# One layer's core kernel: attention rows turned over 128 partitions, two weight quarters loaded into exponential tiles, and an output projection whose last half runs in two groups of four blocks

## The chip, the cores and the metric

The kernel runs on one core of a Trainium2 chip. A core has five engines with an instruction stream each: TensorE (PE) for matrix products, VectorE (DVE), ScalarE (ACT), GpSimd (POOL) and SyncE (SP), which here issues the DMA transfers. The metric is the device time of one execution in microseconds, the median of several runs.

## The reference, cut to what matters

One decoder layer for 1024 tokens of width 1024, float32. One input projection feeds two kinds of heads, four heads each, and their outputs go through one output projection and a squared-ReLU MLP:

```python
h = rms_norm(x, norm1_w)
proj = h @ w_in                     # differential attention q, k, v | DeltaNet q, k, v, gate, a, b
da_q, da_k = per-head rms_norm of 64 columns each (4 heads x 2 maps)
...
s = softmax over the causal keys of q.k / 8, two maps a head
da_o = (s1 - lambda * s2) @ da_v    # per block of 128 queries
...
dn_o = gated delta rule, chunks of 64 tokens, one state a head
mix = concat(da_o, dn_o)            # 512 + 512 columns
x = x + mix @ w_out
h = rms_norm(x, norm2_w)
x = x + square(relu(h @ w_up)) @ w_down
```

## The kernel before, in words

Every large product is made of three matrix products in a rounded float type: an operand is split into a high part (`wH`, `hH`) and a remainder (`wL`, `hL`), and PE adds high by high, high by low and low by high into the same PSUM tile. A matmul of the large stages is 128 x 128 by 128 x 512.

The order in time: the gate projections and the DeltaNet projections (to about 211 us of the span), then a long stretch in which many things run between one another (about 211 to 606 us), then the up projection and the down projection (to the end at 1225 us). The change lies in the long stretch. It holds:

- `horner` and `scan`: the chunked delta rule, with many small matmuls. `horner` keeps four 128 x 1024 tiles in the pool `ae` (four buffers, tag `pexp`; two of these tiles are called `gb` in the profile) until its last step. Its loads from DRAM are `gb`, the scan's are `pka`, `pkb` and `zgt`.
- `da_units`: the projection of the differential attention's queries, keys and values, in three units of 512 columns. A unit goes over the eight blocks of 128 tokens in four pairs, and for each pair over two halves of the 1024 input rows (`kh`); a half is four products deep and each product is three matmuls (lines 1012 to 1014). The tile `ps_qk` of a block is copied out by ACT into `qn` (line 1040; in the units with values also line 1034 or 1035), and POOL and DVE then work out its norms. When the last pair has used a half's weights, `load_unit` fetches the same half of the next unit: four quarters of 128 x 512, each in two DMAs into a tile `wraw`, of which there are two; ACT rounds each to `wH` (line 213) and DVE subtracts to get `wL` (line 214). A third quarter's DMA can therefore be issued only after the first quarter was rounded and subtracted.
- `da_turns`: the normed rows of `qn` are transposed on PE (lines 965 and 966, tile `ps_qkt`), then split into high and low part: for each half of 64 partitions ACT writes the high part into the tile `qa` at these partitions (line 972) and DVE the low part at the other 64 (line 973). Two such steps make one tile, which is written to DRAM (`qk_d`).
- `scores` and `values`: for a head, its keys are loaded from `qk_d` into two tiles `KS` (line 1068, one DMA each), and for each block its queries into `qa` (line 1085, one DMA) and, with the halves swapped, into `qb` (lines 1086 and 1087). PE forms the scores (lines 1148 to 1151), ACT the exponentials (`pexp`, line 1157, from the pool `ae` or, in part after the scan, from a pool `be`), PE turns the result (line 1189) and multiplies it with the values (line 1201).
- `mixed` and `outproj`: the output projection (lines 1291 to 1293). Its half of input rows with the DeltaNet outputs comes first, the half with the attention outputs last; the output columns come in two halves `n`. Blocks become ready one by one, from the last block to the first, since a block needs its attention outputs. For the last half the code keeps a list of (n, block) and takes the first entry that is ready; n = 1 of a block only after its n = 0. After n = 1 of a block comes `norm2`: the sums of squares (line 1310) in a tile `hn` of the pool `ae`, and a DMA `acc_d<-acc` of the block's sum to DRAM (line 1308). The same memory of the block then takes the turned rows (`kept`, line 254) of the first four blocks, and `turn_b` (line 1384) turns the other four. Once every n = 0 is done, `first_ops` loads the first operands of the up projection (`wraw<-in_w_up_dram`, line 1443; rounded at line 1371).

The order of all this is set by a planner (`Interleave`, called `flow`). Each of the above is a stream that yields the time at which it could go on; the planner picks among the streams by priority and keeps a model of the time with fixed costs (`act(n)`, `vec(n)`, `unit_time`, 2500 ns for a DMA). PE executes exactly in the planned order. The instructions of ACT, DVE, POOL and SP are ordered by the compiler's scheduler from the program, and each engine then works strictly down its own list: an instruction that waits holds up all behind it.

Of the kernel before, what the change touches and what calls it, by code (L numbers as in the profile page):

```python
# [18 lines left out]
P = 128  # L19
# [100 lines left out]
def act(n, accum=False):  # L120
    return "S", 55.0 + 0.83 * n + (93.0 if accum else 0.0)
# [11 lines left out]
def tile_hymba_layer(  # L133
# [65 lines left out]
    def load_unit(src, ranges, k0=0, nk=KB, eng=None, rp=None):  # L199
# [6 lines left out]
        for k in range(0, nk, st):  # L206
            raw = rp.tile([P, 2 * UC], F32, tag="wraw", name="wraw", bufs=5) if rp else laid("wraw")
# [563 lines left out]
    def unit_time(eng="G", rate=1230.0):  # L771
        done = []
        for i in range(4):
            start = flow.now if i < 2 else done[i - 2]
            done.append(flow.chain(("S", 520.0), (eng, rate), start=start + DMA_T))
        return done
# [180 lines left out]
    def da_turns():  # L957
        for i in range(4 * NT):
# [11 lines left out]
            for m in range(2):  # L970
                a, b = HF[m], HF[1 - m]
                S.activation(qa[a, m, :], pt[a, 0:256], AF.Copy, scale=wv[a])
                V.scalar_tensor_tensor(qa[b, m, :], pt[a, 0:256], wv[a], qa[a, m, :].bitcast(F32),
                                       ALU.mult, ALU.subtract)
            flow.pe(2 * TR)
            t = flow.chain(act(256), act(256), vec(256, 60), vec(256, 60), start=max(flow.now, qa_free[i % 2]))
            flow.put_off(t, ("qa", i % 2), lambda g=g, kind=kind, tb=tb, qa=qa: nc.sync.dma_start(
                qk_d[g, kind, tb], qa.bitcast(F32).rearrange("p m (h t) -> p m h t", h=2)))
# [8 lines left out]
    def da_units():  # L987
        todo = [[(512, 256), (0, 256)], [(1024, 256), (768, 256)], [(1280, 256), (256, 256)]]

        def half_w(src, ranges, k0):  # L990
            return load_unit(src, ranges, k0, 4, eng=V), unit_time("V", 610.0)
# [3 lines left out]
        for i in range(3):  # L995
            if i == 1:
                vts[0] = ap.tile([P, NT, P], F32, tag="vt", name="vt")
            for pair in range(NT // 2):
                pss = {}
                for kh in range(2):  # L1000
# [19 lines left out]
                    if pair == NT // 2 - 1:  # L1020
                        if i < 2:
                            w[kh] = half_w(w_in_v, todo[i + 1], 4 * kh)
# [41 lines left out]
    def load_head(h, pool):  # L1064
        KS = []
        for m in range(2):
            k = pool.tile([P, SEQ], F32R, tag=f"KS{m}", name=f"KS{m}")
            nc.sync.dma_start(k.bitcast(F32).rearrange("p (b t) -> p b t", t=P),
                              qk_d[h // 2, 1, :, :, m, h % 2, :].rearrange("b p t -> p b t"))
# [11 lines left out]
    def load_q(h, tb):  # L1081
        qa = ap.tile([P, 2, P], F32R, tag="qa", name="qa", bufs=2)
        qb = ap.tile([P, 2, P], F32R, tag="qb", name="qb", bufs=2)
        src = qk_d[h // 2, 0, tb, :, :, h % 2, :]
        nc.sync.dma_start(qa.bitcast(F32), src)
        nc.sync.dma_start(qb[HF[0]].bitcast(F32), src[HF[1]])
        nc.sync.dma_start(qb[HF[1]].bitcast(F32), src[HF[0]])
# [4 lines left out]
    ready = []  # L1092

    def scores():
# [6 lines left out]
        for u, (h, tb) in enumerate(order):  # L1101
# [31 lines left out]
            pl = n // npc  # L1133
            pe, ssum = [], ap.tile([P, 2], F32, tag="ssum", name="ssum", bufs=4)
            mx = ap.tile([P, 2], F32, tag="mx", name="mx", bufs=4)
            for m in range(2):
# [18 lines left out]
                ep = pools["be"] if state["scan"] and npe % 3 == 0 else ae  # L1155
# [699 lines left out]
```

## Time and profile before

| what | value |
|---|---|
| median of 3 runs | 1226.38 us (1225.47 to 1226.53) |
| the profiled execution | 1226.58 us, with a span of 1224.9 us |
| PE busy | 1212.0 us, 99% of the span |
| DVE, ACT, POOL busy | 850.0, 604.6, 121.0 us |
| matrix products, counted by the hardware | 6330 |
| bytes moved by DMA | 199.04 MB, mean 163 GB/s |

The span runs from the first to the last instruction of the profiled execution; the 1.7 us between it and the execution's time lie around it. Busy time of PE counts a matmul from its start to its modelled end, and successive matmuls overlap, so that the sum over the single instructions is larger than PE's busy time. In a list of waits, "PE a <- ACT b: 1.9, 1, 1.9" says that PE stood before instructions on tile a until ACT had written b, for 1.9 us in all, once, at most 1.9 us at a time. The column after POOL in a table of stretches is the TensorE clock that was granted, as a share of the full one; then come the share of the DMA engines' time that is in use, and GB/s.

### The profile page before, as it was taken

The page shows a single profiled execution, that of the slowest core. Times are in us where ns is not written, and L with a number is a line of the kernel's source. Part 1 is how long each engine was busy: PE and PEld are TensorE (multiplying, and loading weights), DVE is VectorE, ACT ScalarE, POOL GpSimd, SP SyncE. Part 2 cuts the span into 40 slices and gives each one's busy share as a digit, 9 for nine tenths or more (in the row PEclk, how much of TensorE's full clock was granted, in tenths as well). Part 3 has the DMA queues.
Part 4 walks back from the last instruction along what each step waited for, and adds up shares of the span by engine and source line. Part 5 has one row for each costly group of instructions (what it writes and reads, how often), then busy time and mean ns, then how long its engine had stood idle before and what let it go on. Part 6 is the DMA issues. An engine that isn't in the chain of part 4 may idle for free.

```text
span 1224.9 us, 17632 instructions
## 1 busy us (share of the span) xinstructions
PE 1212.0 (99%) x6330; PEld 1029.2 (84%) x6330; DVE 850.0 (69%) x1448; ACT 604.6 (49%) x1176; POOL 121.0 (10%) x162
## 2 busy tenths in 40 slices
PE   9999999999999999999999999999999999999998
PEld 9988888898888888888788888888888888888887
DVE  7786788477868577766798554566577955786553
ACT  8565545234556555656666444454554333333331
POOL 0011110223332230212100000000000000000000
PEclk9999999999999999999999999999999999999999
DMA  6564442456755584434528433443279855433301
GB/s 230 176 182 125 112 130 87 116 183 218 241 161 180 173 244 135 115 80 142 183 86 291 155 127 133 170 174 135 103 253 353 325 185 183 160 104 104 138 35 69
DMA packets 161087, 199.04 MB, mean 163 GB/s; under 512 B 21008, under 2 KB 120936, under 8 KB 161000
## 3 DMA queue, kind: packets, MB, share of 16 engines
q1 hardware_dynamic: 160856, 197.79, 49.3%
q8 instruction: 50, 0.82, 0.3%
q14 instruction: 37, 0.30, 0.1%
q10 hardware_dynamic: 144, 0.13, 0.0%
HBM read 132.32 MB, written 65.56 MB: 162 GB/s over the span
## 4 chain that ended last, share of the span: by engine, by line
PE 89%; DVE 4%; DMA 3%; ACT 2%; issue 1%; SPq 0%; POOL 0%; ACTq 0%; DVEq 0%
PE X L1454 5%; PE X L1453 5%; PE X L1452 5%; PE X L1768 4%; PE X L1769 4%; PE X L1770 4%; PE ps_dn L221 4%; PE ps_dn L219 4%; PE ps_dn L220 4%; PE ps_qk L1012 3%; PE Y L1454 3%; PE Y L1453 3%; PE Y L1452 3%; PE ps_qk L1014 3%; PE ps_qk L1013 2%; PE ps_o L1201 2%
## 5 line engine op out<-in xcount | busy, mean ns | idle before, releaser
L1371 ACT CAST hH<-ur 128x1024 fp32r<-128x1024 f32 x56 | 58.6, 1048 | 166.0 <-PE X L1769 79.7
L1372 DVE TENSOR_TENSOR hL<-ur,hH 128x1024 fp32r<-128x1024 f32 x56 | 68.5, 1224 | 79.8 <-ACT hH L1371 79.8
L1372 DVE TENSOR_TENSOR op<-raw,op 128x1024 fp32r<-128x1024 f32 x48 | 58.7, 1223 | 75.3 <-PE X L1453 42.3
L1768 PE MATMUL X<-hH 128*128 128x512 f32 x224 | 87.2, 389 | 0.0
L1769 PE MATMUL X<-hL,hH 128*128 128x512 f32 x224 | 87.2, 389 | 0.0
L1770 PE MATMUL X<-hH,hL 128*128 128x512 f32 x224 | 87.2, 389 | 0.0
L1012 PE MATMUL ps_qk<-wH,hH 128*128 128x512 f32 x192 | 82.2, 428 | 1.9 <-ACT qn L1040 1.9
L1014 PE MATMUL ps_qk<-wH,hL 128*128 128x512 f32 x192 | 75.8, 395 | 0.0
L219 PE MATMUL ps_dn<-hH,wH 128*128 128x512 f32 x192 | 75.7, 394 | 0.0
L220 PE MATMUL ps_dn<-hL,wH 128*128 128x512 f32 x192 | 75.6, 394 | 0.0
L1013 PE MATMUL ps_qk<-wL,hH 128*128 128x512 f32 x192 | 75.4, 393 | 0.1
L221 PE MATMUL ps_dn<-hH,wL 128*128 128x512 f32 x192 | 75.4, 393 | 0.0
L1372 DVE TENSOR_TENSOR hL<-dw,hH 128x1024 fp32r<-128x1024 f32 x56 | 68.2, 1220 | 3.2 <-ACT hH L1371 3.2
L1371 ACT CAST op<-raw 128x1024 fp32r<-128x1024 f32 x48 | 50.4, 1050 | 34.8 <-PE Y L1454 20.1
L1371 ACT CAST hH<-dw 128x1024 fp32r<-128x1024 f32 x56 | 58.6, 1047 | 16.7 <-DMA dw<-in_w_down_dram 5.1
L1157 ACT ACTIVATE pexp<-ps_sc,mx 128x128 f32<-128x128 f32 (+7 forms) x64 | 47.3, 740 | 26.1 <-DVE mx L1153 26.1
L595 DVE SCALAR_TENSOR_TENSOR cy<-cp,pv,cy 128x512 f32<-128x512 f32 x72 | 53.7, 750 | 7.8 <-ACT cy L593 7.0
L1153 DVE TENSOR_REDUCE mx<-ps_sc 128x1 f32<-128x128 f32 (+7 forms) x64 | 47.5, 754 | 14.1 <-PE ps_sc L1151 13.5
L1291 PE MATMUL ps_op<-wH,hH 128*128 128x512 f32 x128 | 53.6, 419 | 0.0
L1293 PE MATMUL ps_op<-wH,hL 128*128 128x512 f32 x128 | 50.3, 393 | 0.0
L1292 PE MATMUL ps_op<-wL,hH 128*128 128x512 f32 x128 | 50.0, 391 | 0.0
L1453 PE MATMUL Y<-hL,op 128*128 128x512 f32 x128 | 49.8, 389 | 0.0
(355 smaller groups left out, 3383.8 us busy)
## 6 DMA issues: line engine op xcount, KB each, us to landing
ur<-ud SPq DMA_DIRECT2D x28, 1024.0 KB, 4.9
raw<-in_w_up_dram SPq DMA_DIRECT2D x32, 512.0 KB, 3.7
dw<-in_w_down_dram SPq DMA_DIRECT2D x32, 512.0 KB, 7.2
qk_d<-qa SPq DMA_DIRECT2D x32, 256.0 KB, 3.1
ud<-ua SPq DMA_DIRECT2D x16, 512.0 KB, 4.0
ud<-s SPq DMA_DIRECT2D x16, 512.0 KB, 3.2
wraw<-in_w_in_dram SPq DMA_DIRECT2D x24, 256.0 KB, 3.5
wraw<-in_w_in_dram SPq DMA_DIRECT2D x48, 128.0 KB, 2.9
```

What stands on the lines that cost most here:

```text
L219: T.matmul(ps, lh(k), rh(k), start=(k == 0), stop=False)
L220: T.matmul(ps, lh(k), rl(k), start=False, stop=False)
L221: T.matmul(ps, ll(k), rh(k), start=False, stop=(k == n - 1))
L1012: T.matmul(ps, hH[:, 4 * kh + k, sl], wh[:, k, :], start=(kh + k == 0), stop=False)
L1013: T.matmul(ps, hH[:, 4 * kh + k, sl], wl[:, k, :], start=False, stop=False)
L1014: T.matmul(ps, hL[:, 4 * kh + k, sl], wh[:, k, :], start=False, stop=(kh + k == 4))
L1371: S.copy(dst[0], src)
L1372: V.tensor_tensor(dst[1], src, dst[0].bitcast(F32), ALU.subtract)
L1453: T.matmul(ps, op[0][:, k, cs], h[1][:, k, :], start=False, stop=False, skip_group_check=True)
L1768: T.matmul(o, v[0][:, j, sl], v[2][:, j, c], start=s0, stop=False, skip_group_check=True)
L1769: T.matmul(o, v[0][:, j, sl], v[3][:, j, c], start=False, stop=False, skip_group_check=True)
L1770: T.matmul(o, v[1][:, j, sl], v[2][:, j, c], start=False, stop=s1, skip_group_check=True)
```

## The change

Three things are edited, and a rule of the planner that goes with them.

First, `da_turns` writes the high part of all 128 rows in one ACT instruction and the low part in one DVE instruction (128 x 256 in place of two 64 x 256 each). The rearrangement that the 64-partition pieces gave is now made when the rows are loaded: `load_head` loads each `KS` in two DMAs of 64 partitions, and `load_q` loads `qa` and `qb` in two DMAs of 64 partitions each, four in place of three.

Second, at the end of unit 0 `load_unit` puts the third and fourth quarter of a half into a tile `more`, taken from the pool `ae` (tag `pexp`), so that these quarters no longer wait for a `wraw` tile. Unit 1's end goes on as before. The planner's `unit_time` is told of four places instead of two for these loads.

Third, the last half of the output projection goes over its list in the order n = 0 of four blocks, n = 1 of these, n = 0 of the other four, n = 1 of these; before, it was n = 0 of all eight and then n = 1 of all. With it goes a count `in_ae` of the tiles that were taken from `ae`, so that `norm2` does not take a tile that still waits to be used.

```diff
--- before.py
+++ after.py
@@ -196,7 +196,7 @@
 
-    def load_unit(src, ranges, k0=0, nk=KB, eng=None, rp=None):
+    def load_unit(src, ranges, k0=0, nk=KB, eng=None, rp=None, more=None):
         eng = eng or G
@@ -204,7 +204,10 @@
         for k in range(0, nk, st):
-            raw = rp.tile([P, 2 * UC], F32, tag="wraw", name="wraw", bufs=5) if rp else laid("wraw")
+            if more is not None and k > 1:
+                raw = more[:, 512 * (k - 2):512 * (k - 1)]
+            else:
+                raw = rp.tile([P, 2 * UC], F32, tag="wraw", name="wraw", bufs=5) if rp else laid("wraw")
             raw = raw[:, :st * width].rearrange("p (k c) -> p k c", k=st)
@@ -768,10 +771,10 @@
 
-    def unit_time(eng="G", rate=1230.0):
+    def unit_time(eng="G", rate=1230.0, ring=2):
         done = []
         for i in range(4):
-            start = flow.now if i < 2 else done[i - 2]
+            start = flow.now if i < ring else done[i - 2]
             done.append(flow.chain(("S", 520.0), (eng, rate), start=start + DMA_T))
@@ -967,15 +970,12 @@
             wv = qw if kind == 0 else kw
-            for m in range(2):
-                a, b = HF[m], HF[1 - m]
-                S.activation(qa[a, m, :], pt[a, 0:256], AF.Copy, scale=wv[a])
-                V.scalar_tensor_tensor(qa[b, m, :], pt[a, 0:256], wv[a], qa[a, m, :].bitcast(F32),
-                                       ALU.mult, ALU.subtract)
+            S.activation(qa[:, 0, :], pt[:, 0:256], AF.Copy, scale=wv)
+            V.scalar_tensor_tensor(qa[:, 1, :], pt[:, 0:256], wv, qa[:, 0, :].bitcast(F32), ALU.mult, ALU.subtract)
             flow.pe(2 * TR)
-            t = flow.chain(act(256), act(256), vec(256, 60), vec(256, 60), start=max(flow.now, qa_free[i % 2]))
+            t = flow.chain(act(256), vec(256, 60), start=max(flow.now, qa_free[i % 2]))
             flow.put_off(t, ("qa", i % 2), lambda g=g, kind=kind, tb=tb, qa=qa: nc.sync.dma_start(
-                qk_d[g, kind, tb], qa.bitcast(F32).rearrange("p m (h t) -> p m h t", h=2)))
+                qk_d[g, kind, tb], qa.bitcast(F32).rearrange("p x (h t) -> p x h t", h=2)))
             qa_free[i % 2] = t + DMA_T
@@ -987,8 +987,8 @@
 
-        def half_w(src, ranges, k0):
-            return load_unit(src, ranges, k0, 4, eng=V), unit_time("V", 610.0)
+        def half_w(src, ranges, k0, more=None):
+            return load_unit(src, ranges, k0, 4, eng=V, more=more), unit_time("V", 610.0, 2 if more is None else 4)
 
@@ -1019,7 +1019,8 @@
                         if i < 2:
-                            w[kh] = half_w(w_in_v, todo[i + 1], 4 * kh)
+                            more = ae.tile([P, SEQ], F32, tag="pexp", name="more") if i == 0 else None
+                            w[kh] = half_w(w_in_v, todo[i + 1], 4 * kh, more)
                         elif kh == 0:
@@ -1065,8 +1066,9 @@
-            nc.sync.dma_start(k.bitcast(F32).rearrange("p (b t) -> p b t", t=P),
-                              qk_d[h // 2, 1, :, :, m, h % 2, :].rearrange("b p t -> p b t"))
+            kv = k.bitcast(F32).rearrange("p (b t) -> p b t", t=P)
+            for x in range(2):
+                nc.sync.dma_start(kv[HF[x]], qk_d[h // 2, 1, :, HF[m], x, h % 2, :].rearrange("b p t -> p b t"))
             KS.append(k)
@@ -1081,15 +1083,15 @@
-        src = qk_d[h // 2, 0, tb, :, :, h % 2, :]
-        nc.sync.dma_start(qa.bitcast(F32), src)
-        nc.sync.dma_start(qb[HF[0]].bitcast(F32), src[HF[1]])
-        nc.sync.dma_start(qb[HF[1]].bitcast(F32), src[HF[0]])
+        parts = [qk_d[h // 2, 0, tb, :, x, h % 2, :].rearrange("(m r) t -> r m t", m=2) for x in range(2)]
+        for t, swap in ((qa, 0), (qb, 1)):
+            for x in range(2):
+                nc.sync.dma_start(t[HF[x]].bitcast(F32), parts[x ^ swap])
         return qa, qb
 
     order = [(0, t) for t in range(NT)] + [(1, t) for t in range(NT)]
     order += [(h, t) for t in reversed(range(NT)) for h in (2, 3)]
-    ready = []
+    ready, in_ae = [], [0]
 
@@ -1131,6 +1133,7 @@
             pl = n // npc
+            mine = []
             pe, ssum = [], ap.tile([P, 2], F32, tag="ssum", name="ssum", bufs=4)
@@ -1153,6 +1156,8 @@
                 ep = pools["be"] if state["scan"] and npe % 3 == 0 else ae
+                mine.append(in_ae[0] if ep is ae else 1e9)
+                in_ae[0] += ep is ae
                 e = ep.tile([P, SEQ], F32, tag="pexp", name="pexp")
@@ -1167,7 +1172,7 @@
             q = load_q(*order[u + 1]) if u + 1 < len(order) and order[u + 1][0] // 2 < state["da"] else None
-            ready.append((h, tb, pe[0], ri, vt, t))
+            ready.append((h, tb, pe[0], ri, vt, t, mine[0]))
         state["scored"] = True
@@ -1303,6 +1308,7 @@
             hn = ae.tile([P, SEQ], F32, tag="pexp", name="hn2")
+            in_ae[0] += 1
             hn = [hn[:, 0:512], hn[:, 512:1024]]
@@ -1336,13 +1342,13 @@
-        todo = [(n, i) for n in range(2) for i in range(NT)]
+        todo = [(n, i) for g in range(2) for n in range(2) for i in range(4 * g, 4 * g + 4)]
         left0 = NT
         flow.add(6, up_first())
         flow.add(4.5, backs())
         while todo:
             j = next((j for j, (n, i) in enumerate(todo) if landed.get((tiles[i], 0), 1e12) <= flow.now
-                      and (n == 0 or (0, i) not in todo) and (n == 0 or state["scored"] and i < 4 or state["free"])), None)
+                      and (n == 0 or (0, i) not in todo) and (n == 0 or state["free"] or state["scored"] and i < 4 and all(in_ae[0] - 4 < x[6] for x in ready))), None)
             if j is None:
```

PE has the same matmuls of the same shapes after the change as before (5826 rows of instructions in both programs); their order differs from the middle of the `horner` stage on. Three places of the programs are shown here.

SP's list in the `horner` and `scan` stages: the loads for the scan's chunks (`pka`, `pkb`, `zgt`) in the program before.

```order
L839 DMA pka<-park_d 128x384 x4
L894 DMA pkb<-park_d 128x256 x4
L896 DMA zgt<-zg_d 128x512
L894 DMA pkb<-park_d 128x256
L839 DMA pka<-park_d 128x384 x4
L894 DMA pkb<-park_d 128x256 x4
L839 DMA pka<-park_d 128x384 x4
L896 DMA zgt<-zg_d 128x512
```

And after:

```order
L897 DMA pkb<-park_d 128x256 x4
L899 DMA zgt<-zg_d 128x512
L897 DMA pkb<-park_d 128x256
L214 DMA more<-in_w_in_dram 128x256 x3
L842 DMA pka<-park_d 128x384 x4
L214 DMA more<-in_w_in_dram 128x256 x5
L897 DMA pkb<-park_d 128x256 x4
L842 DMA pka<-park_d 128x384 x4
L899 DMA zgt<-zg_d 128x512
```

The eight transfers of the two `more` tiles (two quarters for each of two halves) stand around the chunk's `pka`, long before the `wraw` transfers of the same weights.

ACT's list at the end of unit 0, before: `wH_3476` is the first half of unit 1's weights, `wH_3619` the second, and `qn` at line 1040 the copy of a finished block.

```order
L213 CAST wH_3476<-wraw 128x512 [waits PE_49]
L213 CAST wH_3476<-wraw 128x512
L972 ACTIVATE qa<-ps_qkt,qw 64x256 [waits DVE_49]
L1040 ACTIVATE qn<-ps_qk,rt 128x512 [waits PE_49,Pool_49]
L213 CAST wH_3476<-wraw 128x512 [waits DMAHW1_49,DMAHW0_49]
L213 CAST wH_3476<-wraw 128x512 [waits DMAHW3_49,DMAHW2_49]
L972 ACTIVATE qa<-ps_qkt,pv 64x256 [waits DMAHW7_49,PE_49,Activation_49]
L972 ACTIVATE qa<-ps_qkt,qw 64x256 [waits DMAHW4_49,DVE_49,PE_49]
L972 ACTIVATE qa<-ps_qkt,pv 64x256 [waits DVE_49]
L919 ACTIVATE osq,so<-oc,small_73 128x128 [waits DVE_49]
L1040 ACTIVATE qn<-ps_qk,rt 128x512 [waits PE_49,Pool_49]
L213 CAST wH_3619<-wraw 128x512 [waits DMAHW1_49,DMAHW0_49]
```

The same place after (line numbers 216 and 1041 for 213 and 1040):

```order
L216 CAST wH_3459<-wraw 128x512 [waits PE_49]
L216 CAST wH_3459<-wraw 128x512
L216 CAST wH_3459<-more 128x512 x2
L973 ACTIVATE qa<-ps_qkt,pv 128x256 [waits DMAHW3_49,DVE_49,PE_49]
L973 ACTIVATE qa<-ps_qkt,qw 128x256 [waits DMAHW4_49,DVE_49,PE_49]
L1041 ACTIVATE qn<-ps_qk,rt 128x512 [waits PE_49,Pool_49] x2
L216 CAST wH_3566<-wraw 128x512 [waits DMAHW4_49,DMAHW3_49]
L216 CAST wH_3566<-wraw 128x512 [waits DMAHW6_49,DMAHW5_49]
L216 CAST wH_3566<-more 128x512
L216 CAST wH_3566<-more 128x512 [waits DMAHW0_49]
L922 ACTIVATE osq,so<-oc,small_73 128x128 [waits DVE_49,Activation_49]
```

The two quarters in `more` are rounded without a wait for a DMA of their own and ahead of the two last copies `qn`; before, the quarters three and four, with waits for two DMAs each, stood between these copies. The three steps on 64 partitions have become two on 128.

ACT's list at the end of the output projection, before: `kept` is the turned block of the first four, `wH_7198` and `wL_7207` are the first operands of the up projection, `hn` the squares of `norm2`.

```order
L1310 ACTIVATE hn_7293,nss<-acc 128x512 [waits DVE_49,Activation_49]
L1310 ACTIVATE hn_7247,nss<-acc 128x512 [waits DVE_49]
L1371 CAST wL_7207<-wraw 128x4x128 [waits DMAHW1_49]
L1310 ACTIVATE hn_7321,nss<-acc 128x512 [waits DVE_49,PE_49,Activation_49]
L1371 CAST wL_7207<-wraw 128x4x128 [waits DMAHW2_49]
L254 COPY kept<-ps_tr 128x512 [waits DMAHW3_49,DVE_49]
L256 CAST hH<-ps_tr 128x4x128
L254 COPY kept<-ps_tr 128x512
L256 CAST hH<-ps_tr 128x4x128
```

The same place after:

```order
L257 COPY kept<-ps_tr 128x512 [waits PE_49]
L259 CAST hH<-ps_tr 128x4x128
L1316 ACTIVATE hn_7239,nss<-acc 128x512 [waits DVE_49,Activation_49]
L257 COPY kept<-ps_tr 128x512 [waits DMAHW4_49,PE_49]
L259 CAST hH<-ps_tr 128x4x128
L257 COPY kept<-ps_tr 128x512 [waits PE_49]
L259 CAST hH<-ps_tr 128x4x128
L257 COPY kept<-ps_tr 128x512 [waits DMAHW5_49,PE_49]
L259 CAST hH<-ps_tr 128x4x128
L1377 CAST wH_7171<-wraw 128x4x128 [waits PE_49,Pool_49]
L1377 CAST wH_7171<-wraw 128x4x128 [waits DMAHW0_49]
L257 COPY kept<-ps_tr 128x512 [waits PE_49]
```

Before, the last pair of `kept` copies, with its wait for a DMA, stood behind both roundings of `wL` and between the squares of the last blocks; after, the copies of all four blocks stand ahead of them and of most squares, and only the two roundings of `wH` come between the last two copies.

More of the change, by code (lines that the diff above doesn't have):

```diff
@@ L1178, in values @@
                 yield (flow.now + 100 if not ready else ready[0][5]), None
-            h, tb, pe, ri, vt, _t = ready[0]
+            h, tb, pe, ri, vt, _t, _ = ready[0]
             while v_at.get(tb, 1e12) > flow.now:
```

## The prediction

> **What bounds the kernel now.** I read the page first: the span, the busy share of each engine, and the slices.
>
> ```profile
> span 1224.9 us, 17632 instructions
> PE 1212.0 (99%) x6330; PEld 1029.2 (84%) x6330; DVE 850.0 (69%) x1448; ACT 604.6 (49%) x1176; POOL 121.0 (10%) x162
> ```
>
> PE is busy for all but 12.9 us of the span, and no other engine comes near. The change takes no matmul away, so it can gain only in two ways: by PE's idle time, or by time in which PE ran at a lower clock. The next view is the table of stretches, for where this time lies (PE's busy time is the first column after the length).
>
> ```profile
> 225.00:425.00 200.00, 196.29 (x1263) 169.81 (x1262) 145.98 (x384) 98.00 (x273) 56.12 (x65) 0.99 0.63 191
> 425.00:600.00 175.00, 171.83 (x999) 148.92 (x998) 123.17 (x263) 101.49 (x260) 36.59 (x47) 1.00 0.46 140
> 600.00:612.00 12.00, 10.88 (x58) 8.75 (x57) 9.75 (x21) 9.44 (x23) 2.00 (x3) 1.00 0.76 260
> 625.00:1225.00 600.00, 596.62 (x2655) 494.84 (x2653) 383.38 (x371) 260.75 (x264) 0.00 (x0) 1.00 0.46 165
> ```
>
> The edits act between the end of the key products and the start of the up projection. There PE idles for 3.71 + 3.17 + 1.12 = 8.0 us. That, and one stretch at a low clock, is all that there is to win; the 600 us behind are as full as they can be. The list of waits of PE (total, times, longest) names what the idle time went to.
>
> ```profile
> PE ps_qk L1012 <- ACT qn L1040: 1.9, 1, 1.9
> PE ps_sc L1148 <- ACT pexp L1157: 1.4, 2, 0.9
> PE ps_tr L1384 <- DVE hL L257: 1.1, 1, 1.1
> ...
> PE ps_at L1189 <- DVE pexp L1167: 1.0, 1, 1.0
> PE ps_at L1189 <- DVE hL L260: 0.6, 2, 0.4
> ```
>
> The largest is a single wait. The timelines of SP, ACT and PE around it (start, length, idle before and releaser) show it to be a DMA in disguise.
>
> ```profile
> 297.99 1.96 SPq L211 DMA_DIRECT2D wraw<-in_w_in_dram  x4
> ```
>
> ```profile
> 298.32 0.69 ACT L1040 ACTIVATE qn<-ps_qk,rt 128x512 f32<-128x512 f32 x1 [0.59 <-PE ps_qk L1014]
> 303.87 1.34 ACT L213 CAST wH<-wraw 128x512 fp32r<-128x512 f32 x2 [4.86 <-DMA wraw<-in_w_in_dram]
> 305.12 0.47 ACT L972 ACTIVATE qa<-ps_qkt,pv 64x256 fp32r<-64x256 f32 x1
> ...
> 308.05 0.69 ACT L1040 ACTIVATE qn<-ps_qk,rt 128x512 f32<-128x512 f32 x1
> ```
>
> ```profile
> 306.26 0.39 PE L1013 MATMUL ps_qk<-wL,hH 128*128 128x512 f32 x1
> 306.49 0.39 PE L1014 MATMUL ps_qk<-wH,hL 128*128 128x512 f32 x1
> 308.79 0.50 PE L1012 MATMUL ps_qk<-wH,hH 128*128 128x512 f32 x1 [1.91 <-ACT qn L1040]
> ```
>
> ACT stood from 299.01 to 303.87 before a rounding, because the third and fourth quarter's DMAs could be issued only at 297.99, when the first two quarters had left the `wraw` tiles. The copy `qn` stood behind those roundings and the turning steps after them, and PE could not open the next block before it. Start to start PE took 308.79 - 306.49 = 2.30 us where 0.23 is usual (306.26 to 306.49): 2.07 us lost. And it goes on, as the clock column of the stretches shows (third from the right).
>
> ```profile
> 306.00:309.00 3.00, 1.09 (x5) 0.59 (x5) 2.84 (x7) 1.91 (x5) 0.71 (x1) 1.00 0.78 214
> 309.00:313.00 4.00, 4.00 (x17) 3.58 (x17) 3.90 (x8) 2.85 (x10) 2.34 (x3) 0.58 0.55 181
> ```
>
> Right behind the gap the granted clock is 0.58 for 4 us: 4 x (1 - 0.58) = 1.7 us more. The Trainium skill (page "TensorE: Matmul & The Clock Gate", Part 1, on the hardware activity monitor) has the clock halved after an idle window of about 3.4 us that runs freely. By that alone a gap of 1.9 us need not cost any clock, the 1.7 us would be no sure part of the stall, and the forecast would be 1223.7; the row shows the drop, and I keep it in the sum.
>
> **The change part by part.** *The weights in `more`.* Quarters three and four no longer wait for `wraw`. In ACT's list both last `qn` copies of unit 0 now stand ahead of every rounding that waits for a transfer of the second half, so the 1.91 us wait should go: 2.07 + 1.7 = 3.8 us. The lower end is 0 (the copy held up by something else), the upper end 3.8; I take all of it, since the rows name one cause. What it costs: eight DMAs on SP of 128 KB, placed around a chunk's `pka` loads.
>
> ```profile
> 239.14 0.43 SPq L894 DMA_DIRECT2D pkb<-park_d  x1
> 247.13 2.57 SPq L839 DMA_DIRECT2D pka<-park_d  x4
> 251.89 1.74 SPq L894 DMA_DIRECT2D pkb<-park_d  x4
> 225.00:250.00 25.00, 24.60 (x209) 20.98 (x208) 14.44 (x34) 3.25 (x9) 5.04 (x5) 1.00 0.47 129
> ```
>
> SP sat idle from 239.57 to 247.13 and from 249.70 to 251.89, and DMA was in use for 0.47 of that stretch. Three issues of about 0.49 us (1.96 / 4 above) ahead of the `pka` and five behind add up to 3.9 us in these two holes of 9.7 us. What is queued behind is `pka`, then `pkb`; if the three wait for the horner's tiles, `pka` comes up to 1.5 us later (three issues). I take 0: the cover is SP's idle time and the scan's distance. If that cover were gone, the scan would come 1.5 us later and PE would meet it in its fixed order, so 0 to 1.5.
>
> *The turned rows.* 64 ACT and 64 DVE steps become 32 each.
>
> ```profile
> L972 ACT ACTIVATE qa<-ps_qkt,pv x32: 456/469/472, 261.5 to 393.9; 64x256 fp32r<-64x256 f32 x32
> ```
>
> The transfers, by the page's list (KB each, us to landing), and two loads of one block on SP:
>
> ```profile
> qa<-qk_d SPq DMA_DIRECT2D x32, 128.0 KB, 2.6
> qb<-qk_d SPq DMA_DIRECT2D x64, 64.0 KB, 2.8
> KS<-qk_d SPq DMA_DIRECT2D x8, 512.0 KB, 5.3
> ```
>
> ```profile
> 339.89 0.58 SPq L1086 DMA_DIRECT2D qb<-qk_d  x1
> 340.52 0.59 SPq L1087 DMA_DIRECT2D qb<-qk_d  x1
> ```
>
> A 128 x 256 step should take what the 64 x 256 takes (469 ns), and at most the 687 ns of the 128 x 512 copy above: ACT is relieved of 32 x 0.469 = 15.0 us, at least 32 x (0.938 - 0.69) = 8 us, and DVE of much the same. Both idle elsewhere, so this is worth nothing by itself; a turn ends about 1 us earlier. The price is on the loads: 32 + 8 = 40 more issues on SP, at 0.6 us each (339.89 to 340.52), 24 us in some 300 in which these loads run. Behind them wait `v_d`, `pkb` and the next block's queries. A block's queries come 0.6 us later, a head's keys by about two issues of 0.5 us, unless a smaller transfer lands sooner. Bounds for a half `KS` of 256 KB on 64 partitions: from below the `qb` row (2.8), from above the whole tile (5.3); the `qa` and `qb` rows say that half the bytes on half the partitions land no sooner, so I am near the upper one. No PE wait on `KS`, `qa` or `qb` stands in the list above, and PE's list has much the same work between a turn and the first score as before, so I cost it 0, from 0 to 32 x 0.6 = 19 us. That 19 is the worst bound of all, and it is a rival below.
>
> The Trainium skill (page "SBUF — State Buffer", section "Door 1: The DMA port swizzle") says that 64 partitions reach 8 of the 16 ports, and have about half the bandwidth. That speaks against the two-piece loads; the `qa` and `qb` rows agree, and by it a `KS` piece would take as long as the tile it halves.
>
> *The order at the end.* The third wait of the list, 1.1 us, stands at the first `turn_b`. ACT's timeline and the chain of waits:
>
> ```profile
> 603.91 0.62 ACT L1371 CAST wL<-wraw 128x512 fp32r<-128x512 f32 x1 [1.74 <-DMA wraw<-in_w_up_dram]
> ...
> 606.04 0.59 ACT L254 COPY kept<-ps_tr 128x512 f32<-128x512 f32 x1 [0.38 <-DMA acc_d<-acc]
> ```
>
> ```profile
> 601.44 4.53 DMA acc_d<-acc
> ```
>
> The fourth block's sum was stored only at 601.44, took 4.53 us, and the last `kept` waited for it. After the change all four blocks have their n = 1 and their store before the other four blocks' n = 0 begins, which is 4 x 12 x 0.23 = 11 us of matmuls; the 4.5 us lie beside them and the 1.1 us go. What is late next: n = 0 of the last block now ends nearer to the first up product, so the up projection's first weights have less room, and in ACT's list the two `wL` roundings, each with a wait for a DMA, stand ahead of the squares of three blocks. ACT waited 1.74 us at such a rounding before (603.91). Bounds for PE: 0 and the 1.1 us just saved; I take 0.5.
>
> *The new plan.* From the middle of `horner` on PE's order differs, so the other waits in the list (1.4 + 1.0 + 0.6 = 3.0 us, and small ones) are dealt anew. Nothing says which way; 0, from -2 to +2.
>
> Sum: 3.8 + 1.1 - 0.5 = 4.4 us. The profiled execution took 1226.58 us (its span and 1.7 around it), 0.2 over the median of the runs; 1226.4 - 4.4 = 1222.0 us.
>
> **The rivals.**
>
> *The stall only moves.* The ring of two stays at the end of unit 1, and for the first two quarters of each half. The chain of waits passes through such a load there too:
>
> ```profile
> 383.65 3.80 DMA wraw<-in_w_in_dram
> ```
>
> If the new order puts a `qn` behind such a wait, PE stands some 2 us and the clock falls once more, 3.8 us lost: 1225.8. For it: same loads, same lists in strict order. Against: before, that place cost PE nothing in its list of waits.
>
> *Queries come late.* Each of the 32 blocks waits for a fourth load. This one ends on the other side.
>
> ```profile
> 364.13 2.28 DMA qa<-qk_d
> ```
>
> For it: this load stands in the chain that ended last, so at least one block had no room. If PE loses 0.6 us at a block, seven blocks use up the gain (4.4 / 0.6), and from twelve on the kernel is slower by over 2.5 us; at half of the 32 it is 16 x 0.6 = 9.6 us, and the time 1222.0 + 9.6 = 1231.6. Against: no PE wait for it before, and queries are asked for one block ahead.
>
> *More goes than I count.* The relieved ACT and DVE and the turn that ends sooner could halve the 3.0 us and take the 0.5: 1222.0 - 2.0 = 1220.0. For it: in the list three of these waits end with ACT or DVE. Against: the plan fits PE's order to the costs it assumes, so that slack is spent again.
>
> **How the numbers follow.** 0.2% (2.5 us) is about what a measurement of this kernel can tell from no change: faster is below 1223.9, slower above 1228.8. The forecast, 1222.0 with its own 1220.8 to 1223.9: 0.50. More goes (below 1220.8): 0.18. The stall moves, or the tail takes the gain (1223.9 to 1228.8): 0.20. Late queries: 0.12. So faster 0.68, same 0.20, slower 0.12. The range takes in the middle cases' prices: from 1218.5, all of the 3.0 and the 0.5 gone, to 1227.0, the first rival with the 1.2 us of two late blocks; it leaves out most of the late queries and a little at the lower end, under 0.2.
>
> **What would show it.** Right, if the list of waits of PE has no `ps_qk` behind `qn` near 305 us, the granted clock is 1.00 in every stretch from 225 on, `ps_tr` at the first `turn_b` waits less than 0.5 us, and PE's idle time between 225 and 625 falls by 2 to 3 us. Wrong, if PE has waits on `KS`, `qa` or `qb`, if a gap of about 2 us stands at another unit's end with a clock under 1 behind it, or if `pka` is waited for near 260 us. The turning steps should read 128x256, x32, near 0.47 us.

## The result, and the profile after

The changed kernel took 1231.76 us (median of 6 runs, 1228.11 to 1233.18), the kernel before 1226.05 us in the same series: a ratio of 1.0040, with a 95% interval of 1.0027 to 1.0053. It is slower by 0.4%, where 0.36% faster was forecast. In a second series (`after_again`, below) the ratio was 1.0067 (1.0054 to 1.0080), so that the two intervals do not overlap: the size of the loss is not the same in every series, its sign is. The runs of the changed kernel spread over 5 us, those of the kernel before over little more than 1 in that series; this belongs to the result and is taken up below.

The page and the stretches of the changed kernel's profile, in the columns of those of before; the tail's stretch runs to 630 us, since its wait has moved there:

```profile
span 1230.2 us, 17609 instructions
PE 1212.5 (99%) x6330; PEld 1030.3 (84%) x6330; DVE 829.5 (67%) x1416; ACT 590.8 (48%) x1144; POOL 123.5 (10%) x162
```

```profile
225.00:425.00 200.00, 194.40 (x1257) 169.50 (x1256) 130.32 (x360) 87.17 (x251) 60.01 (x67) 0.98 0.65 189
425.00:600.00 175.00, 169.35 (x984) 146.40 (x983) 115.31 (x249) 97.85 (x248) 35.07 (x45) 1.00 0.46 136
600.00:630.00 30.00, 28.68 (x144) 23.65 (x144) 25.64 (x48) 19.65 (x40) 2.16 (x4) 1.00 0.60 193
630.00:1230.00 600.00, 596.91 (x2656) 494.99 (x2655) 383.42 (x371) 260.78 (x264) 0.00 (x0) 1.00 0.46 165
```

DVE has lost 20.5 us of work and ACT 13.8, and PE works as long as before. Its idle time before the up projection has grown from 8.0 to 5.60 + 5.65 + 1.32 = 12.6 us; the 600 us behind are unchanged. The waits of PE say on what (total, times, longest):

```profile
PE ps_sc L1152 <- DMA qb<-qk_d: 2.4, 1, 2.4
PE ps_sc L1151 <- DMA qa<-qk_d: 2.3, 2, 2.0
PE ps_at L1194 <- DVE ri L1169: 2.2, 1, 2.2
PE ps_sc L1151 <- ACT pexp L1162: 1.9, 3, 0.9
PE ps_tr L1390 <- ACT hn L1391: 1.3, 1, 1.3
```

The wait of `ps_qk` on `qn` is gone. In its place stand four new ones. The chain of waits gives the story of the first, at 372.6 us (start, length, what):

```profile
364.39 4.34 DMA wraw<-in_w_in_dram
...
368.81 0.63 ACT wH L216
369.46 0.04 DVE wL L217
...
371.18 1.30 DVE pexp L1172
...
372.63 0.63 PE ps_at L1194 x4
```

This is the end of unit 1, where the two `wraw` tiles still serve four quarters. The fourth quarter landed at 368.7; ACT rounded it, DVE, whose list stood at the subtraction of that quarter, could only then go on to the exponentials of the attention, and PE could not turn them. It is the stall that the change removed at unit 0's end, by another door. The second, at 408 us, is a load of queries; the chain's rows, and three of SP's timeline:

```profile
401.88 5.99 DMA qa<-qk_d
...
407.96 0.53 PE ps_sc L1151
```

```profile
396.77 1.28 SPq L1071 DMA_DIRECT2D KS<-qk_d  x2
...
399.24 0.58 SPq L1071 DMA_DIRECT2D KS<-qk_d  x1
...
402.57 2.35 SPq L1089 DMA_DIRECT2D qb<-qk_d  x2
```

A transfer of 64 KB, which takes 2.8 us in the median, took 5.99 behind the pieces of a `KS`. It could not have been issued earlier: the chain has SP release it at 401.45, when PE had finished the scores that used the same tile, so some 4.5 us were left before PE asked for it at 405.9. SP itself was held up: two issues in 2.35 us in place of 1.2, and its list of waits has a row that the kernel before has not (the queries' issues, waiting for landings of `KS`):

```profile
SPq L1089 <- DMA KS<-qk_d: 3.8, 5, 1.2
```

The third, at 515 us, is again a load of queries. It was issued late, behind a load of weights that waited for POOL's subtraction of the quarter before, and took 4.29 us where 2.4 is the median:

```profile
505.73 2.54 POOL wL L217 x2
508.26 0.50 SPq L214
...
510.74 4.29 DMA qb<-qk_d
...
515.07 0.41 PE ps_sc L1152
```

The fourth, at 625 us, is the tail, taken up with the order of the last half. Behind the first two gaps the clock fell, behind the third it did not (third column from the right):

```profile
374.00:378.00 4.00, 4.00 (x14) 3.35 (x13) 2.26 (x7) 1.90 (x5) 2.06 (x3) 0.58 0.29 82
409.00:412.00 3.00, 3.00 (x11) 2.62 (x10) 1.51 (x3) 0.74 (x3) 0.00 (x0) 0.58 0.25 71
516.00:520.00 4.00, 4.00 (x28) 3.65 (x27) 3.12 (x8) 2.12 (x6) 0.55 (x1) 1.00 0.46 131
```

### The profile page after: what moved, and what is told of

It reads as the page before. It is cut to its first block, busy times and chain, and to the rows that moved or that the text cites. A ratio compares the mean times of both kernels' runs of the same rounds, so it can differ in the third digit from the quotient of the medians.

```text
span 1230.2 us, 17609 instructions
## 1 busy us (share of the span) xinstructions
PE 1212.5 (99%) x6330; PEld 1030.3 (84%) x6330; DVE 829.5 (67%) x1416; ACT 590.8 (48%) x1144; POOL 123.5 (10%) x162
## 4 chain that ended last, share of the span: by engine, by line
PE 91%; DMA 4%; DVE 2%; issue 1%; ACT 1%; SPq 1%; POOL 1%; ACTq 0%; POOLq 0%
PE X L1459 5%; PE X L1458 5%; PE X L1460 5%; PE X L1776 4%; PE X L1774 4%; PE X L1775 4%; PE ps_dn L222 4%; PE ps_dn L224 4%; PE ps_dn L223 4%; PE ps_qk L1012 3%; PE ps_qk L1014 3%; PE ps_qk L1013 3%; PE Y L1459 2%; PE Y L1458 2%; PE Y L1460 2%; PE Z L1776 2%
## 5 line engine op out<-in xcount | busy, mean ns | idle before, releaser
L1458 PE MATMUL Y<-hH,op 128*128 128x512 f32 x128 | 49.8, 389 | 0.0
```

Source lines behind the costliest of these rows:

```text
L1458: T.matmul(ps, op[0][:, k, cs], h[0][:, k, :], start=start and k == 0, stop=False, skip_group_check=True)
```

## The experiments

Theory 1: two causes of their own, the loads in pieces (408 and 515 us) and the `wraw` ring at unit 1's end (372 us). Its rival: PE's new order asks for things too early, whoever brings them. To hold the order fixed, the planner is told the changed kernel's costs wherever the text says that PE's list is the same; then only the loads and steps differ. Each was timed against the kernel before on the same chip; ratios are to it.

| kernel | us | ratio, 95% interval |
|---|---|---|
| undo_turns | 1229.25 | 1.0024 (1.0014 to 1.0035) |
| ring_u1 | 1225.90 | 1.0000 (0.9984 to 1.0015) |
| undo_turns_ring_u1 | 1227.99 | 1.0018 (1.0009 to 1.0028) |
| undo_order | 1229.91 | 1.0028 (1.0018 to 1.0038) |
| loads2 | 1225.67 | 0.9990 (0.9982 to 0.9999) |
| loads2_ring_u1 | 1220.93 | 0.9956 (0.9944 to 0.9968) |
| more_alone | 1226.72 | 1.0003 (0.9994 to 1.0012) |
| turns_alone | 1230.54 | 1.0035 (1.0023 to 1.0047) |
| loads2_ring_undo_order | 1218.95 | 0.9942 (0.9930 to 0.9954) |
| loads2_q4 | 1229.18 | 1.0020 (1.0010 to 1.0030) |
| loads2_ks4 | 1228.16 | 1.0017 (1.0005 to 1.0028) |
| after_again | 1234.24 | 1.0067 (1.0054 to 1.0080) |
| best_no_more0 | 1222.72 | 0.9967 (0.9955 to 0.9979) |

Differences in us are taken from the 1231.76 of the first series, unless another base is named. The four runs whose names begin with `undo_` or `ring_` were timed on the same chip as `after_again`; from its 1234.24 they are larger: 5.0 us for undo_turns, 8.3 for ring_u1, 6.3 for both together, 4.3 for undo_order. Between runs on different chips (loads2, loads2_ring_u1, more_alone and turns_alone on one, loads2_q4, loads2_ks4, loads2_ring_undo_order on that of `after_again`, best_no_more0 on a third) the ratios are the safer figures.

**The ring at unit 1's end** (ring_u1).

```diff
-more = ae.tile([P, SEQ], F32, tag="pexp", name="more") if i == 0 else None
+more = ae.tile([P, SEQ], F32, tag="pexp", name="more") if i == 0 else accs[NT - 1 - kh]
```

> The changed kernel, and at the end of unit 1 too the third and fourth quarter go into a tile of their own (a row tile of the residual sum that is not filled yet), the planner told nothing of it, PE's list the same. Theory 1 (ring): the 2.2 us wait at 372 us comes from the fourth quarter, which landed at 368.8 us because a wraw tile came free late, held ACT's rounding, then DVE's subtraction and the exponentials behind it; then it goes, with the 1.7 us of low clock behind it: 1231.8 - 3.9 = 1228. Theory 2: DVE's list is too full there anyway, and the wait only shrinks by what DVE idled, under 1 us: 1231.

1225.90: 5.9 us less than the changed kernel, more than the 3.9 expected. The stretch of that wait is full:

```profile
350.00:375.00 25.00, 25.00 (x137) 21.48 (x136) 18.68 (x45) 17.53 (x45) 8.06 (x10) 1.00 0.69 189
```

The wait at 408 us shrank with it to 0.8 us, and no low clock followed it; but in this profile the clock fell behind the waits at 506 us (2.0) and in the tail (2.2), so these rows do not add up to the 5.9. The ring is a cause of its own all the same, and theory 2 is out; loads2 against loads2_ring_u1 below, both on one chip, says so too (4.7 us). But the runs spread from 1222.16 to 1233.11: with a mean granted clock of 1.000 they took 1222.2 to 1223.5 us, with 0.997 1226.8 to 1229.5, with 0.994 1233.1.

**The turning steps and loads of before** (undo_turns), then with the ring's edit (undo_turns_ring_u1).

```diff
-S.activation(qa[:, 0, :], pt[:, 0:256], AF.Copy, scale=wv)
...
+for m in range(2):
+    a, b = HF[m], HF[1 - m]
+    S.activation(qa[a, m, :], pt[a, 0:256], AF.Copy, scale=wv[a])
...
```

> The changed kernel with the turning steps and the loads of before (two steps on 64 partitions, one transfer for a KS, three for a block's queries), while the planner is told the new costs, so that PE's list is the changed kernel's, row for row. Theory 1 (loads): the waits of PE at 408 us (2.0, queries that took 6 us beside the four KS pieces) and at 515 us (2.4, queries issued late) come from the added transfers on SP; then both go, with the low clock behind the first, and the time falls from 1231.8 to about 1226 (2.2 + 1.7 + 2.4 = 6.3 us less at most, 4 at least). Theory 2 (place): PE's new list asks for these queries too early for any load; then the waits stay with half a microsecond less each, and the time stays at 1230 to 1232.

> Both of the two edits before, PE's list the changed kernel's. If loads and ring are two causes of their own, their gains add up: 1231.8 - 6 - 3.9 = about 1222, below the kernel before. If one removed wait only brings out the next, it ends within 1.5 us of the better of the two, 1224.5 or more.

1229.25 and 1227.99: 2.5 and 3.8 us, less than half of what was expected. From `after_again` the first is 5.0 us, as expected, but the two together, 6.3, are less than the ring alone. So the gains do not add up. The waits for queries at 408 and 515 us did go, as theory 1 says. Others came, and some of them are for the half steps or for what stands behind them (undo_turns, whose profile is of its fastest run, 1226.95):

```profile
PE ps_o L1208 <- DVE qa L976: 1.0, 1, 1.0
PE ps_qkt L968 <- ACT at L1198: 0.9, 2, 0.7
```

Here the experiment changed two things: fewer loads, and 32 more steps each on ACT and DVE, in a plan made for fewer. The next one keeps the steps.

**Whole loads with the new steps** (loads2), and with the ring's edit (loads2_ring_u1). The rows lie in DRAM in the order (piece, row, map), so that one transfer over 128 partitions loads what two did; a turned tile is written in two.

```diff
-qk_d = dram.tile([2, 2, NT, P, 2, 2, P], F32, name="qk_d")
+qk_d = dram.tile([2, 2, NT, 2, 64, 2, 2, P], F32, name="qk_d")
...
+nc.sync.dma_start(qa.bitcast(F32), src.rearrange("x r m t -> (x r) m t"))
+nc.sync.dma_start(qb[HF[0]].bitcast(F32), src[1])
+nc.sync.dma_start(qb[HF[1]].bitcast(F32), src[0])
```

> The changed kernel with its turning steps on 128 partitions, but the rows lie in DRAM so that a KS is loaded in one transfer and a block's queries in three, as before; the price is two writes per turned tile in place of one. PE's list is the changed kernel's. Theory 1 (loads): the waits for queries at 408 and 515 us go without the burden that the half steps put on ACT and DVE: 1231.8 - 3.9 - 2.5 = about 1225.5. Theory 2 (SP's list): what matters is the number of transfers on SP as a whole, 32 more writes for 40 fewer loads, so the waits only move: 1229 or more.

> The same with the third and fourth quarter of unit 1's end in a tile of their own too. Theory 1: from 1225.9 (that ring alone) less the waits for queries still in its profile (2.0 + 0.8) and what they do to the clock: 1221 to 1223, below the kernel before by 0.3%. Theory 2: 1225 to 1226, no better than the ring alone.

1225.67 and 1220.93, both as theory 1 had it. PE's longest wait for queries in loads2 is now

```profile
PE ps_sc L1152 <- DMA qb<-qk_d: 0.7, 1, 0.7
```

With the same list of PE, the same steps and the same bytes, whole loads make 1.0040 into 0.9990; with the ring it is 0.9956, clear of the kernel before. It is not the number of transfers on SP as a whole that counts: there are 40 loads fewer, but 32 writes more. And undo_turns_ring_u1 against loads2_ring_u1 (1.0018 against 0.9956, the same PE list, the same number of loads) puts the faster turning steps at some 7 us in this plan, which was made for their costs. That figure is in part argued: the two kernels also differ in the order of the rows in DRAM and in the 32 writes, and of the 6.2 us by which PE idles longer between 225 and 640 us, 2.2 are waits that name the half steps themselves.

**Which loads** (loads2_q4: queries in four again; loads2_ks4: each `KS` in two again).

```diff
-nc.sync.dma_start(qa.bitcast(F32), src.rearrange("x r m t -> (x r) m t"))
+for x in range(2):
+    nc.sync.dma_start(qa[HF[x]].bitcast(F32), src[x])
```

> The kernel with whole loads (1225.7), but a block's queries in four transfers again, KS whole; PE's list the same. If the fourth transfer of the queries is what hurts: the waits for queries are back at 408 and 515 us, 1229 to 1231. If it is the KS pieces that queries wait behind: the one at 408 stays away, and the time is within 1.5 us of 1225.7.

> The kernel with whole loads, but each KS in two transfers of 64 partitions, queries in three; PE's list the same. If the KS pieces hurt: the wait at 408 us is back with its low clock, 1225.7 + 3.9 = 1229 to 1230. If not: 1225 to 1227.

Each costs by itself: +3.5 and +2.5 us on loads2, to 1.0020 and 1.0017, with nothing changed but these loads. The wait at 515 us is back with the queries' fourth transfer alone (and the exponentials at 368 us come 2.3 us late):

```profile
PE ps_sc L1153 <- DMA qb<-qk_d: 2.0, 1, 2.0
```

With the `KS` pieces alone it is not, but the exponentials at 369 us come 3.4 us late:

```profile
PE ps_sc L1152 <- ACT pexp L1163: 5.1, 3, 3.4
```

The wait at 408 us was back in neither (0.6 us at most). As far as these two profiles go it needs both: the queries' fourth transfer behind the pieces of a `KS`, as in the changed kernel. So neither expectation held in full.

**One part alone** (more_alone, turns_alone, made by putting the other parts back as before). Here PE's order is planned anew.

> The kernel before with the third and fourth quarter of unit 0's end in the exponential tiles, turning steps, loads and the order of the output projection as before; 211 rows of PE's list differ from before. By the prediction's first term: 1226.2 - 3.8 = 1222.4. If the wait and the low clock only move to another place of the new plan: 1225.5 to 1227.

> The kernel before with the turning steps on 128 partitions and the loads in pieces alone; weights and output projection as before. If the loads in pieces carry the loss: 1226.2 + 2 to 6, so 1228 to 1232, with PE waits on queries or KS in the profile. If they are hidden, as the prediction had it: 1226 within 1.

The tiles for the weights alone: 1.0003, nothing. PE's wait moved from 307 to 312 us and grew, with the clock at half behind it. Its timeline, ACT's and DVE's:

```profile
312.30 0.30 PE L968 MATMUL ps_qkt<-ident,qn 128*128 128x128 f32 x1 [2.55 <-DVE qa L976]
```

```profile
304.78 0.47 ACT L975 ACTIVATE qa<-ps_qkt,qw 64x256 fp32r<-64x256 f32 x1 [2.77 <-DMA qk_d<-qa]
```

```profile
308.75 0.75 DVE L1061 TENSOR_TENSOR qn<-qn,rn 128x256 f32<-128x256 f32 x2
309.42 1.28 DVE L217 TENSOR_TENSOR wL<-more,wH 128x512 fp32r<-128x512 f32 x2
...
311.66 0.49 DVE L976 SCALAR_TENSOR_TENSOR qa<-ps_qkt,qw,qa 64x256 fp32r<-64x256 f32 x1
```

ACT first stood before a half step until the write of an earlier turned tile had landed, which made what DVE had to do behind it late. The four subtractions then come almost in one go, and the half step of a turn, on whose PSUM tile PE waits, comes behind them. The steps and loads alone: 1.0035, nearly the whole loss, with PE waits of 2.3 us on `qb` and 0.8 on `KS`, but not by the loads alone. A third wait, at 392 us, goes back along its chain to weights that landed late at the end of unit 1, where the ring still has two places:

```profile
PE ps_o L1206 <- DVE qa L974: 2.0, 1, 2.0
```

No run has the order of the last half alone.

**The order of the last half** (undo_order on the changed kernel; loads2_ring_undo_order on the best).

```diff
-todo = [(n, i) for g in range(2) for n in range(2) for i in range(4 * g, 4 * g + 4)]
+todo = [(n, i) for n in range(2) for i in range(NT)]
```

> The changed kernel with the list of the output projection's last half in the order of before; 28 rows of PE's list differ, all behind 550 us. Theory: the order only trades one wait at a turn of the later blocks (1.1 us before, at 608 us) for another (1.3 us, at 625 us); then no change, 1231.8 within 1 us. Rival: the groups of four are worth the 1.1 us or cost as much: 1230.5 or 1233.

> The kernel with whole loads and both unit ends in tiles of their own, and the output projection's list in the order of before. In the profile with the new order PE waits 2.4 us at a turn of the later blocks at 613 us (a copy behind a rounding of the up projection's weights, which waits 3.7 us for a wraw tile and its transfer), and the clock falls to 0.60 for 3 us behind it. Theory: the new order causes this, since it brings the up product nearer to its weights; with the old order 1 us or less is waited there and the clock stays: 1220.9 - 1.5 - 1.5 = about 1218. Rival: the old order has its own 1.1 us and more, as before: 1220 to 1221.

On the changed kernel 1229.91 against 1231.76, or against 1234.24 on the same chip (1.0028 against 1.0067, intervals apart); and 1218.95 against 1220.93 where nothing else disturbs, with ratios of 0.9942 against 0.9956, whose intervals overlap a little. So the old order is worth some 2 to 4 us. With the new order a turn of the later blocks waits behind a rounding of the second weights of the up projection, whose transfer comes late. ACT's timeline, the stretch behind it, DVE's and SP's timelines in loads2_ring_u1:

```profile
611.74 0.62 ACT L1377 CAST wH<-wraw 128x512 fp32r<-128x512 f32 x1 [3.74 <-DMA wraw<-in_w_up_dram]
```

```profile
613.00:616.00 3.00, 3.00 (x11) 2.47 (x12) 2.69 (x6) 2.96 (x7) 0.00 (x0) 0.60 0.00 0
```

```profile
604.39 1.29 DVE L1378 TENSOR_TENSOR wH<-wraw,wH 128x512 fp32r<-128x512 f32 x2
```

```profile
603.41 4.14 SPq L1436 DMA_DIRECT2D raw<-in_w_up_dram  x2
607.65 1.01 SPq L1449 DMA_DIRECT2D wraw<-in_w_up_dram  x2
```

```profile
SPq L1436 <- DMA acc_d<-acc: 7.8, 3, 3.3
```

DVE had done with both `wraw` tiles at 605.7, but the load stood in SP's list behind the `raw` loads of the up projection. These go into a block's own row tile, and had to wait for that block's store `acc_d`, the last of them 3.3 us. So it is SP's list, more than the two tiles, that makes these weights late. With the old order PE waits 0.8 us at that turn, and the clock stays:

```profile
PE ps_tr L1390 <- DVE hL L260: 0.8, 1, 0.8
```

This kernel is the fastest of all. Its stretches:

```profile
225.00:425.00 200.00, 199.33 (x1298) 174.37 (x1298) 131.22 (x366) 89.10 (x255) 61.72 (x69) 1.00 0.68 194
425.00:600.00 175.00, 170.96 (x996) 148.40 (x995) 121.65 (x261) 102.22 (x262) 34.20 (x44) 1.00 0.49 147
```

0.67 us of idle time in 200 where the kernel before has 3.71; its five runs lie within 2 us.

**The first term by itself** (best_no_more0: the fastest kernel with the late quarters of unit 0's end back in the ring).

```diff
-more = ae.tile([P, SEQ], F32, tag="pexp", name="more") if i == 0 else accs[NT - 1 - kh]
+more = None if i == 0 else accs[NT - 1 - kh]
```

> The fastest kernel so far (turning steps on 128 partitions, whole loads, a tile of their own for the late quarters at the end of unit 1, old order of the output projection; 1218.95), with the late quarters at the end of unit 0 back in the two wraw tiles; PE's list the same row for row. If the prediction's first term holds where nothing else is late: a wait of PE of about 2 us near 305 us with the low clock behind it, 1219 + 2 to 3.8 = 1221 to 1222.7. If the faster turning steps alone had already freed ACT's list: 1219 within 0.7.

0.9967 against 0.9942: the tiles are worth 0.25%, 3.1 us, in the range that was expected. The form differs: two waits of about 1 us each, at 330 us and 303 us, and no low clock.

```profile
PE ps_sc L1151 <- DMA KS<-qk_d: 1.0, 1, 1.0
PE ps_qk L1013 <- ACT qn L1042: 0.9, 1, 0.9
```

**The spread** (after_again, the changed kernel unaltered).

> The changed kernel once more, on the same chip as the three others, for its spread (1228.1 to 1233.2) and a second profile. If the spread is the clock that falls behind some of its gaps in some runs and not in others, the time of a run goes with its mean granted clock, about 1.2 us for each 0.001, from about 1228 at 1.000; if it is the transfers that land at other times, runs of one clock spread as widely.

1234.24, all five runs at a clock of 0.996 or 0.997, and still from 1232.8 to 1236.9. So both are true: the clock falls in three places here (behind the gaps at 408, 512 and 626 us, not behind that at 373), and the transfers land at other times. The gap before the queries of that block (ended at 515 us with the clock untouched in the first profile, at 512 here) shows now:

```profile
512.00:516.00 4.00, 3.60 (x18) 3.48 (x19) 2.72 (x6) 2.02 (x5) 1.21 (x1) 0.73 0.31 90
516.00:520.00 4.00, 4.00 (x21) 3.53 (x20) 0.81 (x4) 1.23 (x4) 0.55 (x1) 0.85 0.36 135
```

## Why the prediction was wrong, step by step

*The weights in `more`, 3.8 us: right in place and nearly in size, wrong as something that stands alone.* The wait at 307 us and the low clock behind it are gone in the changed kernel, and the tiles undone alone in the fastest kernel cost 3.1 us. The eight loads that they add did no harm that the list of waits shows: PE does not wait for `pka`. Added alone to the kernel before the tiles bring nothing, since the half steps of the turns come late next. The prediction asked what is late next at the output projection, but not here.

*The turned rows, "worth nothing by itself": wrong.* The steps take what was said (0.47 us for 128 x 256, 32 steps in place of 64), and ACT and DVE idle elsewhere. But in their strict lists they stand between PE's PSUM tiles and the next work of PE, and with the same PE list their speed is put at some 7 us (undo_turns_ring_u1 against loads2_ring_u1, with the two other differences named there). Idle time of an engine says nothing of the wait at one place in its list.

*The loads, "I cost it 0": the step that failed.* The added transfers cost 0.5% (loads2 against the changed kernel), some 6 us where the sum has nothing. The bounds held it, 0 to 19 us; the choice within them did not. It rested on two things: that no such wait was in the list of before, which says nothing of the room left, and that the two PE lists have much the same work ahead of the first score, whereas the waits came much later: at a block of the second head, while the third head's keys were being loaded (408 us), and at a block of the third head (515 us). The rival of late queries had the right cause and the wrong form: not 0.6 us at each of many blocks, but 2.0 and 2.4 us at two, where the queries stood behind `KS` pieces or a load of weights, and 1.7 us of low clock behind one of them. Its chance, 0.12, was too low, also because the load's row in the chain of waits was quoted and then set aside. By the Trainium skill (page "SBUF — State Buffer", section "Door 1: The DMA port swizzle") a transfer on 64 partitions has about half the bandwidth. The trace agrees in its own numbers: a half `KS` of 256 KB took 5.4 us, the whole one 5.3 in the kernel before; no run parts this from the pieces' standing behind one another.

*The order at the end, 1.1 - 0.5: wrong in sign.* The wait of 1.1 us at 608 us went as said, and what was named as late next, the up projection's weights, was priced at 0.5 us by a guess between 0 and 1.1. It measured 1.3 us in the first profile, and 2.4 with a fallen clock in loads2_ring_u1. There the store `acc_d`, which the prediction saw hold up a `kept`, holds up a `raw` load, with these weights behind it in SP's list.

*The new plan, 0 within 2: wrong.* It put the ring's second stall, at unit 1's end, on PE's path: 2.2 us and 1.7 of clock, as the first rival had it and nearly at its price of 3.8, though through DVE's list and the exponentials, not through `qn`. Removed alone it gave 5.9, or 8.3 by the second series, more than its own rows account for.

The two rivals were given chances as if one excluded the other. Both came true at once, and with the tail they outweighed the 3.8 us that the tiles won. An estimate from the rows of the first profile: 2.4 + 2.0 + 1.7 for the loads, 2.2 + 1.7 for the ring, 1.3 - 1.1 for the tail, less 3.8, gives 6.4 us; the medians differ by 5.7.

## What to carry to other kernels

When PE is busy for 99% and follows a fixed order, what remains are a few places where one late transfer holds a strict list; removing one pays only as far as the next entry in the same list is on time, so follow the list on past the removed wait. A load that has never been waited for has no proven room: before it is cut into pieces, measure how long before its use it lands, at its worst place and not at its first. And when a change re-plans the order, test each part with the order held fixed, by giving the planner the same costs; here that turned 0.4% slower into 0.58% faster: the steps and the tiles kept, the loads made whole, one more stall of the same kind removed, and the order put back.

## What the runs showed of the hardware

A gap of about 2 us in PE's work may or may not be followed by some 3.4 us at half the clock (a granted clock of 0.58 over 4 us is 3.4 us at 0.50), in the same program: behind the third wait of the changed kernel the clock stayed at 1.00 in one profile (a wait of 2.4 us) and fell to 0.73 and 0.85 in another (2.0 us). This fits a window that runs freely (the Trainium skill, page "TensorE: Matmul & The Clock Gate", Part 1), though not its length as a need for 3.4 us of idleness: 1.9 us sufficed at 309 us in the kernel before. Over all fifteen profiles, between 225 and 640 us, 15 of the 22 gaps of 1.9 us and more (the longest 3.4) had a fallen clock behind them; no shorter gap had, and the clock fell nowhere else there. This fits the spread of kernels with several such gaps: 5 us in the changed kernel, 11 in ring_u1, 2 in the fastest one, whose profile has no gap over 1.1 us in this part. The clock is not all of the spread: undo_turns_ring_u1 ran from 1226.8 to 1229.2 us with a mean granted clock of 1.000.

SP's issues of loads waited for landings of other loads (3.8 us, five times, on `KS`). The program built from the changed kernel shows where this comes from: SP's transfers count on eight semaphores in turn, and the issue of a transfer waits until the one eight places ahead of it in the list has landed. The two issues of `qb` at 402.57 us stand eight places behind a piece of a `KS` each. So a load cut in two takes two of eight places, and one that lands late can hold SP's whole list. No run varies this.
